# A third tap group on TensorE in a causal convolution, and a bias table written by another queue

## The chip, the cores and the metric

The kernel runs on one core of one Trainium2 chip. The metric is the device time of one execution in microseconds (us); the runs of a kernel are compared by their median. The core has five engines with a queue of instructions each: PE (TensorE, matrix products), DVE (VectorE), ACT (ScalarE), POOL (GpSimd) and SP (which here issues transfers). Each takes its instructions strictly in the order of its queue, and waits on semaphores for what other engines and transfers have to deliver.

## What is computed

Two layers over 256 positions and 2048 channels: a convolution mixer, a feed-forward block with a short causal convolution (FFN), an attention mixer with a relative position bias, and a second FFN. What the change touches is the first mixer and the bias of the attention:

```python
def _conformer_conv(h, w_in, b_in, dw_w, dw_b, ln_g, ln_b, w_out, b_out):
    u = h @ w_in + b_in
    a, gate = jnp.split(u, 2, axis=-1)
    u = a * jax.nn.sigmoid(gate)
    u = _causal_dwconv(u, dw_w, dw_b)            # 31 taps, one filter per channel
    u = jax.nn.silu(_layernorm(u, ln_g, ln_b))
    return u @ w_out + b_out

# in _diff_attention
bucket = _t5_bucket(k_pos[None, :] - q_pos[:, None])
bias = bias_table[:, bucket]
allowed = k_chunk[None, :] <= (q_pos // CHUNK)[:, None]
s = jnp.where(allowed, s + bias[None, :, None], -jnp.inf)
```

All arithmetic is float32. The kernel multiplies by splitting a float32 number into a rounded part (hi) and a rest (lo), and adds three products.

## The kernel before

**Weights.** Every weight matrix is cut into loads of 512 KB. SP's queue brings a load into one of 5 buffers `raw` (L140). ACT writes the rounded copy `hi` (L150), and DVE or POOL the rest `lo` (L152), each with 6 buffers. The splits run four loads ahead of PE. One load feeds one *step* of PE, and a list of steps is the order of the program; `self.at(n, fn)` puts a piece of work n steps later, at the end of that step. Within that, a scheduler that simulates the engines writes the instructions of each queue in order, so the order of the listings below is what runs.

**First mixer** (`conv_module`). 16 tiles of 128 channels; four loads, so four steps, make one tile: 96 matmuls (L217) into a PSUM buffer `pp` (2 of them). When a tile is done, `post` takes it on: DVE multiplies it by the row norm `rstd` into a tile `E` (L436), ACT takes the sigmoid of the gate (L438), DVE multiplies both into the padded tile `cpad` (L440). The 31 taps of the convolution are then shared out. Some go to PE, in groups of four taps: for that the tile must lie in SBUF four times, shifted by one position each. So ACT's queue writes `cpad` to DRAM (`ud`, L452) and reads it back four times (`R`, L456). POOL builds the small diagonal matrices `dg` (L458). `taps` (L475) multiplies them with `R`: 4 matmuls with 32 output rows for each group, side by side in the array, into a PSUM tile `acc` (named s or t). `G` lists how many groups each tile gives to PE: 2 for tiles 0 to 10, then 3, 3, 5, 6; tile 15 goes another way. The taps that are left are steps on DVE (L513), one multiply-add per tap into `acc`, at most six per step of the program and alternating between two tiles where two are open. `dev` (L544) subtracts a mean and keeps the tile for the layernorm, which waits for all 16.

The work on PE of tile i's `taps` is put 4 steps after the tile's end, which is the end of the next tile.

**First FFN, and the set-up of the attention** (`attn_setup`, run at the first step of the FFN). One small matmul makes the bias of all relative positions for 16 heads; DVE copies it to SBUF (L730), and ACT's queue writes it to DRAM 128 times over, 3 MB, as 2048 rows of 384 numbers (`d1`, L732). Each head later reads a skewed window of it (`bm`, L809), from ACT's queue, and POOL sets the masked corner (L810). There are 2 buffers `bm`. In ACT's queue, the reads of the first two heads stand soon after the table's write. In the same stretch the row norm of the FFN is made: POOL takes the power (`rc`, L286), PE turns it into rows (L280), ACT copies them (`rstd`, L348). Each FFN tile is summed up by a copy on ACT (L254) and an addition on DVE (L256), which frees its `pp`.

Of the kernel before, what the change touches and what calls it, by code (L numbers as in the profile page):

```python
# [8 lines left out]
F32 = mybir.dt.float32  # L9
F32R = mybir.dt.float32r  # L10
AF = mybir.ActivationFunctionType
ALU = mybir.AluOpType
AX = mybir.AxisListType
ET = mybir.EngineType
P = 128
S = 256
# [5 lines left out]
MASK = -1.0e30  # L22
# [3 lines left out]
class Cfg:  # L26


    def __init__(self, d, f, kc=4):
        self.D, self.F = d, f  # L30
        self.KT = d // P
        self.FT = f // P
        self.H = d // (2 * HD)
        self.KC = kc
        self.NW = kc * 256
        self.kcs = [(i, kc) for i in range(0, self.KT, kc)]
        full = self.KT // 2
        first = self.FT % full or full
        self.chunks = [(0, first)] + [(i, full) for i in range(first, self.FT, full)]
        self.VK = kc // 2  # L40
        self.NA, self.NB = self.KT + self.KT // 2 + 1, 8

        self.G = [2] * (self.KT - 5) + [3, 3, 5, 6, 0]

        self.ND = 18

# [15 lines left out]
class Builder:  # L62
# [363 lines left out]
    def conv_module(self, nin, nout):  # L426
        c, a = self.c, self.a
# [4 lines left out]

        def post(i, ps):
            with self.tc.high_priority():
                t = self.b2("E")
                nc.vector.tensor_tensor(t, ps[:, :, 0:S], nin["rstd"].unsqueeze(1).to_broadcast([P, 2, S]), ALU.mult)  # L436
                sg = self.b1("G")
                nc.scalar.activation(sg, t[:, 1, :], AF.Sigmoid, bias=self.col("bin", KT + i))  # L438
                u = self.cpad[i % 3]
                nc.vector.scalar_tensor_tensor(u[:, CK - 1:CK - 1 + S], t[:, 0, :], self.col("bin", i), sg, ALU.add,  # L440
                                               ALU.mult)
                if i == KT - 1:
                    nc.scalar.activation(self.c2(), sg[:, 0:2], AF.Silu)
# [11 lines left out]
            for s in range(4):  # L455
# [1 line left out]
            dg = self.ph1.tile([P, 4 * gm, 32], F32, tag="dg", name=self.nm("dg"))[:, :4 * g, :]  # L457
            nc.gpsimd.tensor_tensor(dg, self.cmask.unsqueeze(1).to_broadcast([P, 4 * g, 32]),  # L458
                                    self.col("wq", 4 * sum(c.G[:i]), 4 * g).unsqueeze(2).to_broadcast([P, 4 * g, 32]), ALU.mult)
            self.at(4, lambda: taps(i, u, R, dg))  # L460
            if i == 0:

                for j in range(0, c.ND, 4):
# [255 lines left out]
    def attn_setup(self):  # L719
# [1 line left out]
        nc, c, a = self.nc, self.c, self.a  # L721
        H = c.H
        rb = self.ph2.tile([NB, H], F32, name="rb")
        nc.scalar.dma_start(rb, a["relb"])
        oh = self.b2("Z").rearrange("p a s -> p (a s)")[:NB, :384]
        nc.scalar.dma_start(oh, a["oneh"])
        ps = self.psx("o", [P, 384])
        nc.tensor.matmul(ps[:H, :], rb, oh, start=True, stop=True)
        tb = self.b2("Z").rearrange("p a s -> p (a s)")[:H, :384]
        nc.vector.tensor_copy(tb, ps[:H, :])  # L730
        d1 = self.dr.tile([H, P, 384], F32, name="d1")
        nc.scalar.dma_start(d1, tb.unsqueeze(1).to_broadcast([H, P, 384]))  # L732
        self.bflat = d1.rearrange("h p d -> (h p d)")
        lm = self.c2()
        nc.vector.tensor_tensor(lm[:HD], self.col("lam", 0, 2)[:HD], self.col("lam", 2, 2)[:HD], ALU.mult)
        ps = self.psx("o", [P, 2])
# [12 lines left out]
    def attention(self, nin, nout):  # L749
        c, a = self.c, self.a  # L750
        nc = self.nc
        H, KT = c.H, c.KT
        V, U, O = {}, {}, {}

        def v_group(g, off):
            box = {}
# [47 lines left out]
            self.at(2, lambda: scores(h, q, k, qk))  # L804

        def bias(h):
            bm = self.ph2.tile([P, S], F32, tag="bm", name=self.nm("bm"), bufs=2)
            o = h * P * 384 + P - 1
            nc.scalar.dma_start(bm, self.bflat[o:o + P * 383].rearrange("(p d) -> p d", d=383)[:, :S])  # L809
            nc.gpsimd.memset(bm[0:64, S - 64:], MASK)  # L810
            return bm

        def scores(h, q, k, qk):
            bm = bias(h)
            ps = [self.psx("s", [P, 2, S]) for _ in range(2)]

            comp = [slice(cc * HD, (cc + 1) * HD) for cc in range(2)]
# [64 lines left out]
        for h in range(H):  # L882
            if h % 4 == 0:
                voff = v_group(h // 4, voff)
            off = self.pair(a["w_qk"], off, c.kcs, lambda k: nin["xh"][k], lambda ps, h=h: qk_post(h, ps))
        off = 0
        held = []
        for pr in range(KT // 2):
# [146 lines left out]
```

## Time and profile before

| | |
|---|---|
| median of 3 runs | 2296.82 us (2295.39 to 2298.47) |
| the profiled execution | 2303.02 us, of which the span from first to last instruction is 2300.4 us |
| busy share of the span | PE 97%, DVE 73%, ACT 52%, POOL 12% |
| the chain that ended last | PE 88%, DMA 5%, DVE 4%, issue 1% |

The busy share of PE is an upper bound of the work in it, since matmuls are pipelined and overlap. The chain is followed back from the last instruction to what released each step; its DMA share is time in which the end of the program waited for transfers. "PEclk" is the clock granted to PE as a share of 2.4 GHz.

### The profile page before, as it was taken

What the parts mean: (1) busy time and instruction counts of PE and PEld (TensorE: products, weight loads), DVE (VectorE), ACT (ScalarE), POOL (GpSimd) and SP (SyncE); (2) the same over time, 40 slices, a digit from 0 to 9 for tenths busy, and PEclk for the clock granted to TensorE, in tenths of its full rate; (3) what the DMA queues carried; (4) which work ended last, traced back from release to release, by engine and by line L of the source; (5) the groups of instructions that cost most, each with busy time, mean ns of one, the idle gap of its engine ahead of it and who ended that gap; (6) DMA issues with size and microseconds to landing.
All of it is one profiled execution on the core that took longest, in us unless ns stands there. A gap on an engine that the chain in (4) does not pass through costs nothing.

```text
span 2300.4 us, 34637 instructions
## 1 busy us (share of the span) xinstructions
PE 2224.6 (97%) x13294; PEld 1947.9 (85%) x13294; DVE 1670.9 (73%) x2539; ACT 1205.7 (52%) x1788; POOL 281.4 (12%) x189
## 2 busy tenths in 40 slices
PE   6899799799999999999999999999999999999998
PEld 6788688688888888888888888888888888888887
DVE  5788876577777767677766777677777777676774
ACT  5333265455555555455655555555555555554554
POOL 5678510000000000000111011010000000000002
PEclk9999899899999999999999999999999999999999
DMA  6766356766666666666655555466666666666663
GB/s 230 195 193 190 111 159 179 191 198 187 190 188 188 187 188 190 188 190 188 188 179 159 168 168 166 140 200 183 189 188 190 186 190 185 191 187 190 189 187 100
DMA packets 126885, 417.15 MB, mean 181 GB/s; under 512 B 14176, under 2 KB 28288, under 8 KB 126720
## 3 DMA queue, kind: packets, MB, share of 16 engines
q1 hardware_dynamic: 110736, 398.30, 56.8%
q10 hardware_dynamic: 15984, 16.65, 3.5%
q8 instruction: 104, 1.70, 0.3%
q14 instruction: 61, 0.50, 0.1%
HBM read 407.44 MB, written 7.45 MB: 180 GB/s over the span
## 4 chain that ended last, share of the span: by engine, by line
PE 88%; DMA 5%; DVE 4%; issue 1%; ACTq 0%; ACT 0%; POOL 0%; POOLq 0%; SPq 0%; DVEq 0%
PE pp L226 47%; PE pp L227 24%; PE pp L224 4%; PE pp L217 3%; PE pp L223 2%; DMA R<-ud 2%; DMA ud<-cpad 2%; DMA d<-Z 2%; PE pp L774 1%; PE pp L775 1%; PE pp L776 1%; DVE s L513 1%; DVE cpad L440 1%; PE s L475 0%; ACTq L456 0%
## 5 line engine op out<-in xcount | busy, mean ns | idle before, releaser
L226 PE MATMUL pp<-act,hi 128*128 128x512 f32 x3902 | 1382.9, 396 | 21.1 <-DVE E L256 13.0
L227 PE MATMUL pp<-act,lo 128*128 128x256 f32 x3902 | 1096.5, 281 | 0.0
L150 ACT CAST hi<-raw 128x1024 fp32r<-128x1024 f32 x752 | 787.6, 1049 | 536.0 <-PE pp L226 179.3
L152 DVE TENSOR_TENSOR lo<-raw,hi 128x1024 fp32r<-128x1024 f32 x686 | 844.3, 1231 | 283.0 <-ACT hi L150 281.2
L226 PEld LDWEIGHTS pp<-act,hi 128*128 128x128 f32 x3902 | 733.3, 188 | 182.9 <-DVE E L256 13.3
L227 PEld LDWEIGHTS pp<-act,lo 128*128 128x128 f32 x3902 | 739.1, 189 | 10.4
L226 PE MATMUL pp<-actb,hi 128*128 128x512 f32 x856 | 306.7, 396 | 0.0
L227 PE MATMUL pp<-actb,lo 128*128 128x256 f32 x856 | 240.4, 281 | 0.0
L321 POOL TENSOR_TENSOR ssq<-ssq,Z 128x512 f32<-128x512 f32 x24 | 35.6, 1481 | 1532.1 <-ACT Z L317 1532.0
L217 PE MATMUL pp<-act,hi 128*128 128x256 f32 x1088 | 209.3, 294 | 11.4 <-ACT act L267 6.0
L217 PEld LDWEIGHTS pp<-act,hi 128*128 128x128 f32 x1088 | 178.0, 200 | 19.3 <-DVE act L268 6.6
L226 PEld LDWEIGHTS pp<-actb,hi 128*128 128x128 f32 x856 | 160.6, 188 | 38.3 <-issue 0.6
L152 POOL TENSOR_TENSOR lo<-raw,hi 128x1024 fp32r<-128x1024 f32 x66 | 159.4, 2434 | 56.0 <-ACT hi L150 52.4
L256 DVE TENSOR_TENSOR E<-pp,E 128x512 f32<-128x512 f32 x104 | 71.8, 690 | 128.2 <-ACT E L254 127.9
L227 PEld LDWEIGHTS pp<-actb,lo 128*128 128x128 f32 x856 | 161.5, 189 | 0.2
L217 PE MATMUL pp<-act,lo 128*128 128x256 f32 x544 | 158.4, 291 | 2.8 <-DVE lo L152 2.8
L254 ACT COPY E<-pp 128x512 f32<-128x512 f32 x104 | 60.8, 585 | 186.9 <-PE pp L224 161.6
L370 ACT COPY E<-pp 128x512 f32<-128x512 f32 x109 | 63.9, 586 | 169.5 <-PE pp L224 161.8
L677 DVE SCALAR_TENSOR_TENSOR Y<-fpad,prm,Y 128x256 f32<-128x256 f32 x352 | 146.7, 477 | 0.0
L372 DVE TENSOR_TENSOR x<-pp,x 128x512 f32<-128x512 f32 x101 | 69.7, 690 | 89.4 <-ACT E L370 89.0
L674 ACT ACTIVATE Y<-fpad,prm 128x256 f32<-128x256 f32 x176 | 96.3, 596 | 48.2 <-DVE fpad L670 48.2
L513 DVE SCALAR_TENSOR_TENSOR s<-cpad,cprm,s 128x256 f32<-128x256 f32 x214 | 97.5, 482 | 24.8 <-PE s L475 22.6
(218 smaller groups left out, 1890.8 us busy)
## 6 DMA issues: line engine op xcount, KB each, us to landing
raw<-in_w_up_dram SPq DMA_DIRECT2D x352, 512.0 KB, 4.0
raw<-in_w_down_dram SPq DMA_DIRECT2D x176, 512.0 KB, 4.0
raw<-in_w_in_dram SPq DMA_DIRECT2D x64, 512.0 KB, 4.5
raw<-in_w_qk_dram SPq DMA_DIRECT2D x64, 512.0 KB, 3.6
raw<-in_w_out_dram SPq DMA_DIRECT2D x32, 512.0 KB, 4.1
raw<-in_w_v_dram SPq DMA_DIRECT2D x32, 512.0 KB, 3.7
raw<-in_w_o_dram SPq DMA_DIRECT2D x32, 512.0 KB, 3.7
R<-ud ACTq DMA_DIRECT2D x44, 130.0 KB, 5.1
```

The source lines that it names most:

```text
L150: nc.scalar.copy(hi[:, :n], raw[:, :n])
L152: eng.tensor_tensor(lo[:, :n], raw[:, :n], hi[:, :n].bitcast(F32), ALU.subtract)
L217: nc.tensor.matmul(ps[:, 0:S], w[:, kk, cs], xt[:, x, :], start=(k == first and n == 0), stop=(k == last and n == 2))
L224: nc.tensor.matmul(*main, start=False, stop=True)
L226: nc.tensor.matmul(*main, start=(k == first), stop=False)
L227: nc.tensor.matmul(*corr, start=False, stop=False)
L256: nc.vector.tensor_tensor(t, ps[:, :, 0:S], cs, ALU.add)
L370: nc.scalar.copy(cs, ps[:, :, S:])
L372: nc.vector.tensor_tensor(x, ps[:, :, 0:S], x, ALU.add)
L513: nc.vector.scalar_tensor_tensor(acc, u[:, j:j + S], self.col("cw", i * CK + j), acc, ALU.mult, ALU.add)
L674: nc.scalar.activation(y[:, j, :], u[:, j, FK - 1:], AF.Identity, scale=self.col("fw", ch * FK + FK - 1), bias=self.col("fb", ch))
L677: nc.vector.scalar_tensor_tensor(y[:, j, :], u[:, j, q:q + S], self.col("fw", ch * FK + q), y[:, j, :], ALU.mult, ALU.add)
```

## The change

- `G` becomes 3 for tiles 0 to 12, then 5, 6 (before 2 for tiles 0 to 10): eleven tiles give a third group, four taps, to PE.
- `post` writes the normed projection back into its PSUM tile instead of into `E`; sigmoid and product read it there.
- `taps` of tiles 0 to 13 stand 5 steps after the tile's end, not 4.
- The three transfers of the bias set-up go from ACT's queue to POOL's. The masked corners are written into the table in DRAM, by 16 small transfers of POOL's queue that wait for the table; the 16 memsets of POOL fall away.
- Each head's window `bm` is read by SP's queue, at the first step of the head's own projection, so about one projection before the scores that use it.

```diff
-        self.G = [2] * (self.KT - 5) + [3, 3, 5, 6, 0]
+        self.G = [3] * (self.KT - 3) + [5, 6, 0]
...
         def post(i, ps):
             with self.tc.high_priority():
-                t = self.b2("E")
-                nc.vector.tensor_tensor(t, ps[:, :, 0:S], nin["rstd"].unsqueeze(1).to_broadcast([P, 2, S]), ALU.mult)
+
+                t = ps[:, :, 0:S]
+                nc.vector.tensor_tensor(t, t, nin["rstd"].unsqueeze(1).to_broadcast([P, 2, S]), ALU.mult)
...
-            self.at(4, lambda: taps(i, u, R, dg))
+            self.at(5 if i < KT - 2 else 4, lambda: taps(i, u, R, dg))
...
         rb = self.ph2.tile([NB, H], F32, name="rb")
-        nc.scalar.dma_start(rb, a["relb"])
+        nc.gpsimd.dma_start(rb, a["relb"])
         oh = self.b2("Z").rearrange("p a s -> p (a s)")[:NB, :384]
-        nc.scalar.dma_start(oh, a["oneh"])
+        nc.gpsimd.dma_start(oh, a["oneh"])
...
-        nc.scalar.dma_start(d1, tb.unsqueeze(1).to_broadcast([H, P, 384]))
+        nc.gpsimd.dma_start(d1, tb.unsqueeze(1).to_broadcast([H, P, 384]))
         self.bflat = d1.rearrange("h p d -> (h p d)")
+
+        mk = self.ph2.tile([64, 64], F32, name="mk")
+        nc.gpsimd.memset(mk, MASK)
+        for h in range(H):
+            o = h * P * 384 + P - 1
+            nc.gpsimd.dma_start(self.bflat[o:o + 64 * 383].rearrange("(p d) -> p d", d=383)[:, S - 64:S], mk)
...
         def bias(h):
-            bm = self.ph2.tile([P, S], F32, tag="bm", name=self.nm("bm"), bufs=2)
+            BM[h] = self.ph2.tile([P, S], F32, tag="bm", name=self.nm("bm"), bufs=2)
             o = h * P * 384 + P - 1
-            nc.scalar.dma_start(bm, self.bflat[o:o + P * 383].rearrange("(p d) -> p d", d=383)[:, :S])
-            nc.gpsimd.memset(bm[0:64, S - 64:], MASK)
-            return bm
+            d = nc.sync.dma_start(BM[h], self.bflat[o:o + P * 383].rearrange("(p d) -> p d", d=383)[:, :S])
+            self.tc.keep_in_program_order(d)
 
         def scores(h, q, k, qk):
-            bm = bias(h)
+            bm = BM.pop(h)
...
-            off = self.pair(a["w_qk"], off, c.kcs, lambda k: nin["xh"][k], lambda ps, h=h: qk_post(h, ps))
+            off = self.pair(a["w_qk"], off, c.kcs, lambda k: nin["xh"][k], lambda ps, h=h: qk_post(h, ps),
+                            pre=lambda h=h: bias(h))
```

PE's queue in the middle of the first mixer, before: the last matmuls of one tile (`pp_1581`), the taps of the tile before it, the first matmuls of the next (`pp_1750`).

```order
L217 MATMUL pp_1581<-act_206,hi_1513 128x256 x2
L217 MATMUL pp_1581<-act_206,lo_1514 128x256
L475 MATMUL s_1713<-R_1568,dg_1573 32x256 x8
L217 MATMUL pp_1750<-act_129,hi_1577 128x256 x2
L217 MATMUL pp_1750<-act_129,lo_1578 128x256
```

The same tile's taps (L476 by the new numbering) in the change; `pp_1724` is the tile that before was `pp_1750`, and between its first matmul (`act_129`) and the taps stand 16 rows, which are 24 matmuls.

```order
L217 MATMUL pp_1724<-act_140,lo_1550 128x256
L217 MATMUL pp_1724<-act_140,hi_1549 128x256 x2
L217 MATMUL pp_1724<-act_140,lo_1550 128x256
L476 MATMUL s_1749<-R_1540,dg_1545 32x256 x12
L217 MATMUL pp_1724<-act_150,hi_1604 128x256 x2
```

The taps moved one step of 24 matmuls later, and are 12 matmuls instead of 8. For tile 0 alone they moved by three rows only, since before they already stood in the third tile.

DVE's queue around the end of a tile, before: the normed projection (L436), the product (L440), and tap steps (L513) that alternate between two accumulators.

```order
L513 SCALAR_TENSOR_TENSOR s_1541<-cpad_232,cprm,s_1541 128x256 x7
L436 TENSOR_TENSOR E_1730<-pp_1581,rstd_226 128x512
L513 SCALAR_TENSOR_TENSOR s_1541<-cpad_232,cprm,s_1541 128x256
L513 SCALAR_TENSOR_TENSOR s_1713<-cpad_235,cprm,s_1713 128x256
L513 SCALAR_TENSOR_TENSOR s_1541<-cpad_232,cprm,s_1541 128x256
L440 SCALAR_TENSOR_TENSOR cpad_238<-E_1730,prm,G_1732 128x256
L513 SCALAR_TENSOR_TENSOR s_1713<-cpad_235,cprm,s_1713 128x256
L513 SCALAR_TENSOR_TENSOR s_1541<-cpad_232,cprm,s_1541 128x256
```

The same place in the change (L514 are the tap steps, L437 and L441 the norm and the product).

```order
L514 SCALAR_TENSOR_TENSOR s_1578<-cpad_232,cprm,s_1578 128x256 x15
L437 TENSOR_TENSOR pp_1553<-pp_1553,rstd_226 128x2x256
L514 SCALAR_TENSOR_TENSOR s_1578<-cpad_232,cprm,s_1578 128x256 x2
L441 SCALAR_TENSOR_TENSOR cpad_238<-pp_1553,prm,G_1706 128x256
L514 SCALAR_TENSOR_TENSOR s_1578<-cpad_232,cprm,s_1578 128x256 x2
L545 SCALAR_TENSOR_TENSOR act_1762<-s_1578,prm,mp 128x256
L514 SCALAR_TENSOR_TENSOR s_1749<-cpad_235,cprm,s_1749 128x256 x15
```

A tile's 19 steps now run in one accumulator, 15 before the next tile's end and 4 around it; before, 23 steps ran partly in turn with the next tile's.

ACT's queue at the start of the first FFN, before: the table's write (L732), some splits, the first two window reads (L809), then the copies that free the FFN's `pp` tiles.

```order
L732 DMA d_3950<-Z_3948 2048x1x384
L254 COPY E_4072<-pp_3973 128x512
L150 CAST hi_4116<-raw_4001 128x1024
L150 CAST hi_4138<-raw_4028 128x1024
L739 ACT_TABLE_LOAD
L739 ACTIVATE c_3956<-o_3954 128x2
L150 CAST hi_4160<-raw_4050 128x1024
L150 CAST hi_4201<-raw_4091 128x1024
L809 DMA bm_11322<-d_3950 128x256
L809 DMA bm_11468<-d_3950 128x256
L254 COPY E_4180<-pp_4097 128x512
```

POOL's queue at that place in the change (L733 is the table's write, L286 the row norm's power, L740 the masked corners).

```order
L321 TENSOR_TENSOR ssq_3197<-ssq_3197,Z_3821 128x512
L727 DMA Z_3928<-in_oneh_dram 32x384
L733 DMA d_3934<-Z_3932 2048x1x384
L286 TENSOR_TENSOR rc_3999<-c_4000,mhalf 128x2
L740 DMA d_3934<-mk 64x64 x16
L321 TENSOR_TENSOR ssq_10576<-ssq_10576,Z_10633 128x512
```

The write and everything that waits for it left ACT's queue; in POOL's, the power of the row norm stands right behind the write and ahead of the 16 corners.

## Rows read from the trace of the kernel before

**Rows 1.** The page, the chain that ended last: shares of the span by engine.

```profile
PE 88%; DMA 5%; DVE 4%; issue 1%; ACTq 0%; ACT 0%; POOL 0%; POOLq 0%; SPq 0%; DVEq 0%
```

**Rows 2.** Windows: stretch, length, busy us of PE, PEld, DVE, ACT, POOL, PEclk, DMA, GB/s.

```profile
180.00:240.00 60.00, 54.52 (x487) 51.18 (x485) 50.29 (x104) 21.08 (x24) 51.38 (x27) 1.00 0.68 192
480.00:540.00 60.00, 60.00 (x346) 52.58 (x345) 45.96 (x68) 34.71 (x51) 0.00 (x0) 1.00 0.62 187
1200.00:1300.00 100.00, 100.00 (x573) 83.56 (x572) 74.21 (x158) 56.59 (x122) 9.87 (x15) 1.00 0.56 166
```

**Rows 3.** Waits of PE from 45 to 262 us: total us, times, longest.

```profile
PE s L475 <- DMA R<-ud: 14.0, 7, 4.9
PE t L475 <- DMA R<-ud: 6.0, 3, 2.6
PE s L475 <- issue: 3.2, 1, 3.2
```

**Rows 4.** Windows, tile by tile, where PE's clock was below full.

```profile
58.00:66.00 8.00, 7.24 (x49) 6.05 (x50) 3.43 (x7) 1.04 (x1) 3.93 (x3) 0.63 0.78 248
...
111.00:126.00 15.00, 14.62 (x120) 13.40 (x124) 10.65 (x26) 4.02 (x5) 9.65 (x6) 0.89 0.64 184
...
168.00:182.00 14.00, 13.58 (x108) 13.07 (x109) 10.66 (x24) 3.68 (x4) 9.02 (x6) 0.88 0.65 195
```

**Rows 5.** The chain that ended last, one tile: start us, us, what.

```profile
226.05 0.69 DVE E L436
...
227.57 2.46 DVE cpad L440
230.06 5.11 DMA ud<-cpad
...
236.50 5.34 DMA R<-ud
241.98 3.77 PE s L475 x40
```

**Rows 6.** PE's timeline and chain: taps of two and three groups, cadence, last projection matmul.

```profile
182.62 1.07 PE L475 MATMUL s<-R,dg 128*32 128x256 f32 x16
225.94 1.50 PE L475 MATMUL s<-R,dg 128*32 128x256 f32 x24
257.13 0.28 PE L217 MATMUL pp<-act,lo 128*128 128x256 f32 x1
1129.77 5.74 PE pp L217 x48
```

**Rows 7.** DVE: line L440 (ns min/median/max), and runs of tap steps in its timeline.

```profile
L440 DVE SCALAR_TENSOR_TENSOR cpad<-E,prm,G x16: 478/1362/2453, 44.8 to 263.3; 128x256 f32<-128x256 f32 x16
69.91 10.01 DVE L513 SCALAR_TENSOR_TENSOR s<-cpad,cprm,s 128x256 f32<-128x256 f32 x25
232.30 7.30 DVE L513 SCALAR_TENSOR_TENSOR s<-cpad,cprm,s 128x256 f32<-128x256 f32 x14
```

**Rows 8.** POOL in the first mixer: a wait, and groups of 60 to 240 us by form.

```profile
POOL c L593 <- DVE c L592: 15.0, 1, 15.0
L152 POOL TENSOR_TENSOR lo<-raw,hi 128x1024 fp32r<-128x1024 f32 x48 | 114.9, 2409 | 39.5 <-ACT hi L150 35.9 <-DMA raw<-in_w_in_dram 3.6
```

**Rows 9.** Timelines of ACT, DVE, POOL and PE around the table's write.

```profile
391.33 0.67 ACTq L732 DMA_DIRECT2D d<-Z  x1
427.82 0.59 ACT L254 COPY E<-pp 128x512 f32<-128x512 f32 x1 [25.08 <-DMA d<-Z]
390.76 0.54 DVE L730 COPY Z<-o 16x384 f32<-16x384 f32 x1
400.90 0.70 POOL L286 TENSOR_TENSOR rc<-c,mhalf 128x2 f32<-128x2 f32 x1 [25.41 <-DVE c L285]
404.97 0.61 PE L280 MATMUL o<-ident,rc 128*128 128x128 f32 x4
415.79 0.39 PE L224 MATMUL pp<-actb,hi 128*128 128x512 f32 x1
429.19 0.80 PE L226 MATMUL pp<-act,hi 128*128 128x512 f32 x1 [13.01 <-DVE E L256]
```

**Rows 10.** DMA from 385 to 430 us (write), 397 to 399 and 398.5 to 401.

```profile
d<-Z ACTq DMA_DIRECT2D x1, 3072.0 KB, 35.6
q10 hardware_dynamic: 127, 0.20, 92.8%
raw<-in_w_up_dram SPq DMA_DIRECT2D x2, 512.0 KB, 18.6
```

More of the change, by code (lines that the diff above doesn't have):

```diff
@@ L752, in attention @@
         H, KT = c.H, c.KT
-        V, U, O = {}, {}, {}
+        V, U, O, BM = {}, {}, {}, {}
         def v_group(g, off):
```

## The prediction

> **What bounds the kernel now.** I read the chain that ended last first: 88% of it is PE, so time is won only where PE waits, runs at a lower clock or does more than it must [rows 1]. The windows by stage say where that is. In the FFN and the attention PE is busy in 60.00 of 60 us and 100.00 of 100, at clock 1.00; nothing done to other engines there can help [rows 2]. In the first mixer it is busy in 54.52 of 60 us, while DVE and POOL, at 50.29 and 51.38, are not full either [rows 2]: three engines wait for each other in turn. The waits of PE name the place. From 45 to 262 us it stood idle for 14.0 + 6.0 + 3.2 = 23.2 us, and every one of these eleven waits is ahead of a tile's taps, for the shifted copies R [rows 3]. Its clock adds to that: 0.63, 0.89 and 0.88 of full in three tiles in which PE had just stood still [rows 4], which is 8 x 0.37 + 15 x 0.11 + 14 x 0.12 = 6.3 us of work at full clock that was not done. Together 29.5 us. The second place is the start of the first FFN: after 415.79 + 0.39 us PE is idle for 13.01 us [rows 9].
>
> **The first mixer.** Why R is late can be read along the chain for one tile: norm at 226.05, product until 230.03, ud written by 235.17, four R copies issued and landed by 241.84, taps at 241.98 [rows 5]. That is 15.9 us from the tile's end. Until then PE has one tile of matmuls, 96 x 5.74/48 = 11.5 us, and one set of taps of 1.07 to 1.50 us [rows 6]: 13.0 us at most. It must wait some 2.9 us.
>
> *Later taps.* 24 matmuls more stand ahead of the taps, 24 x 0.12 = 2.9 us, and the set of taps between is 1.50 us: PE gets there 11.5 + 1.5 + 2.9 = 15.9 us after the tile's end. This alone just meets the 15.9 us.
>
> *Norm in PSUM.* The product (L440) reads two tiles in SBUF and takes 478 ns at best, 2453 at worst, 2.46 us in the tile of the chain [rows 5, 7]. A tap step, which also takes one operand from SBUF and one from PSUM, runs in 0.52 us behind its forerunner at the worst [rows 7]. With the projection in PSUM the product is such an instruction; I take 0.48 us, so R comes 2.0 us sooner in such a tile, 13.9 us after its end. The bounds are 0 and 2.0 us. That `pp` is held about 2 us longer costs nothing: the next tile uses the other buffer for 11.5 us.
>
> *What is left of the waits.* 2.0 us of slack stand against more traffic: 192 GB/s with PE busy 54.52 of 60 us becomes about 192 x 60/54.52 = 211 when it is not held [rows 2], and if the 5.11 + 5.34 us of transfers [rows 5] grow in that ratio, 1.0 us of the slack is gone. I leave 0.3 us of wait to each of 11 tiles, 3.3 us. Tile 0 is another matter: its taps moved by three rows, 0.4 us, so of the longest wait, 4.9 us [rows 3], 4.5 us remain, and with them the slow clock behind it, 3.0 us [rows 4]. Gain: 29.5 - 3.3 - 7.5 = 18.7 us. Bounds: 22.0 us without a new wait, and 6.6 if each of 11 tiles waits 1.4 us.
>
> *The third group* costs PE 1.50 - 1.07 = 0.43 us a tile [rows 6], 11 x 0.43 = 4.7 us, all on the path. It takes four tap steps from DVE, but saves DVE little: the 19 that are left all depend on one accumulator, 7.30/14 = 0.52 us each, where alternating ones took 10.01/25 = 0.40 [rows 7]; 19 x 0.52 = 9.9 us. With norm, product and `dev` DVE needs about 11.5 us a tile, and PE 13.0. That is the cover, 1.5 us; were it gone, norms would start late and the taps with them. POOL's larger `dg` (128 numbers more; a split of 1024 takes 2.41 us, so an estimated 0.3 us) hides in the 39.5 us that it was idle ahead of its splits [rows 8]. What follows the last projection matmul (257.13, [rows 6]) moves forward as it is. Sum for the mixer: 18.7 - 4.7 = **14.0 us**, from 2 to 17.
>
> **The start of the FFN.** ACT issues the table's write at 391.33, in 0.67 us. Then its queue comes to the reads of that table, and the copy behind them (L254) starts 25.08 us later than it could, released by the write [rows 9], which takes 35.6 us to land [rows 10]. That copy frees a `pp`, DVE's addition follows, and PE is held 13.01 us; it then restarts with a matmul of 0.80 us against 0.39 [rows 9], and I put 1.5 us of slow clock behind the wait. In the change nothing on ACT waits for the table; PE's next cause of standing still must be looked for. Gain if there is none: **14.5 us**.
>
> What is late next could be POOL. The write now stands in its queue ahead of `rc`, which PE needs for the rows of the norm. Before, POOL took `rc` at 400.90, and PE came to the rows at 404.97 [rows 9]. The table is ready at 391.3, so POOL may spend about 404.97 - 391.3 - 0.8 = 12.8 us on writing out the transfer before PE stands; every us above is lost. No row of before has a transfer issued by POOL. Bounds: 0.67 us, as for ACT [rows 9], and 35.6 us if it were held until all has landed [rows 10]. Nearest is POOL's own pace, 2.41 us for 1024 numbers per partition [rows 8], 2.4 ns each: an estimate of 5 us for 2048 rows at one such unit a row, 19 at four. I take a value under 12.8, cost 0. The Trainium skill speaks against the move: its page "DMA: Bandwidth & Descriptors", section "SWDGE vs HWDGE vs iDMA", says that for transfers issued from GpSimd a program on its cores computes the descriptors, while hardware does it for SP and ACT. The same page of the Trainium skill, section "Anatomy of one DMA", finds that many descriptors come out before their number is felt, by which the cost would be 0; no run here shows either.
>
> The corners come behind `rc`, and POOL has no work from 480 to 540 us [rows 2]. The load of `rb`, new in POOL's queue ahead of the layernorm's power, falls in a wait of 15.0 us [rows 8]. The window reads on SP stand among weight loads and wait for the scores two heads back; weights are split four loads ahead, and PE is never idle there (100.00 of 100, [rows 2]), so 0, and no gain either for ACT and POOL, which are relieved.
>
> **Sum.** 14.0 + 14.5 = 28.5 us. The profiled execution took 2303.0 us, 6.2 above the median of 2296.8; 2303.0 - 28.5 = 2274.5, and on the scale of the median **2268 us**, 1.2% less.
>
> **Rivals.**
>
> *POOL is held by the table's write* for G us, more than 12.8. The time is 2268 + 1.5 + (G - 12.8): 2277 at 20 us, 2292 at 35.6. From 45 us on (22 ns a row) the kernel is slower than before by over 0.2%, which is 4.6 us and about what a measurement can tell; at 60 us it takes 2317. For it: 2048 rows at an unknown price, right ahead of `rc`. Against it: 45 us is longer than the whole transfer now takes, and over nine times POOL's pace per number. 0.12 for 12.8 to 45 us (a third of it within 0.2%), 0.06 for more.
>
> *The wait changes its name.* While the table was written, its queue took 92.8% of the DMA engines, and weight loads landed after 18.6 us [rows 10]. PE did not feel it, since loads already split lasted until it stopped for another reason. If POOL's transfer shuts the loads out for all 35.6 us, the load issued at about 395 lands near 427, its split is ready at 430 and PE, which needs it at about 420, waits 10 us and restarts slowly: some 12 to 13 us of the 14.5 are gone, 2281. Against it: before, the loads came through after 18.6 us. The same page of the Trainium skill has a rule for it, "Issuing engines are not separate DMA queues": moving a transfer to another engine saves only the time of issuing it. By that the FFN gains 0.67 us and the time is 2282; the 25.08 us of ACT were a wait in its queue, not issue, and I hold the rule not to reach it. 0.08.
>
> *The copies stay late.* If ud and R take 3 us longer under the denser traffic, each of 13 tiles waits 1 us more than the slack covers: 13 us, 2281. For it: the DMA engines already show 0.68 of their time busy at 192 GB/s [rows 2]. Against it: the FFN is served at 187 GB/s without a wait of PE. 0.14.
>
> **The numbers.** My forecast has 0.60, with a range of its own of 2260 to 2276. With the rivals: faster by over 0.2% 0.60 + 0.08 + 0.14 + 0.08 = 0.90; within 0.2% 0.04; slower 0.06. The range is 2259 (mixer 17, FFN 14.5, and 6 of the 7.5 us kept for tile 0 gone too) to 2284 (either gain lost nearly whole, or POOL held up to 27 us); above it about 0.1 is left out, below it less.
>
> **What will show it.** Waits of PE ahead of the taps: about 8 us in all instead of 23.2, over half of it in tile 0. The product near 0.48 us. Taps x24 of 1.50 us in nearly every tile, the last projection matmul near 243 us instead of 257. At the FFN no idle PE of 13 us, `rc` at most 4 us later than DVE's input for it, and a POOL row for the write that tells G. Wrong would be: PE idle ahead of the norm's rows (first rival), ahead of a first matmul with a fresh load (second), or still ahead of the taps (third).

## The result, and the profile after

The change takes **2269.08 us** in the median of four runs, the kernel before 2297.64 beside it. Three of the four lie between 2264.77 and 2269.90, with a median of 2268.26; the fourth took 3646.37 at a granted clock of 0.556 and is left out of the ratio, which is 0.987, interval 0.9851 to 0.989. On a second chip it is 0.9866, 0.9847 to 0.9885. It is faster by 1.3%, as forecast in size and sign. But the terms of the sum are not as forecast, and it is worth seeing why two errors gave a right total.

The page of the change, the chain that ended last, shares by engine, where [rows 1] had 88% PE and 5% DMA:

```profile
PE 93%; DVE 2%; DMA 2%; ACT 1%; issue 1%; POOL 0%; SPq 0%; ACTq 0%; POOLq 0%; DVEq 0%
```

Windows of the change, columns as in [rows 2]. The mixer's PE is full now up to the last tiles, and the mixer carries 212 and 213 GB/s, where [rows 2] had 192.

```profile
60.00:120.00 60.00, 59.80 (x551) 55.38 (x550) 50.92 (x107) 22.56 (x27) 50.00 (x27) 1.00 0.73 212
...
180.00:240.00 60.00, 58.25 (x555) 52.94 (x554) 49.49 (x96) 22.67 (x27) 51.16 (x25) 1.00 0.75 213
```

PE's waits ahead of the taps, which in [rows 3] were eleven of 23.2 us, are two of 3.4:

```profile
PE s L476 <- DMA R<-ud: 3.2, 1, 3.2
...
PE s L476 <- issue: 0.2, 1, 0.2
```

PE's longest wait from 45 to 262 us is none of these: 7.35 us ahead of w_out's first matmul, for the end of the layernorm on DVE. It was 7.75 before, so the change leaves it as it was.

PE's timeline of the change. Start, us, what; in brackets idle time ahead and what ended it. Tile 0's taps wait; from the third tile on they come round every 13.14 us, without a wait. The last taps (x48) start at 233.73, right behind the last matmul of the projection, which in [rows 6] stood at 257.13.

```profile
43.09 0.51 PE L217 MATMUL pp<-act,hi 128*128 128x256 f32 x2 [0.78 <-DVE cpad L441]
54.58 1.70 PE L476 MATMUL s<-R,dg 128*32 128x256 f32 x24 [3.19 <-DMA R<-ud]
...
130.44 1.50 PE L476 MATMUL s<-R,dg 128*32 128x256 f32 x24
143.58 1.50 PE L476 MATMUL s<-R,dg 128*32 128x256 f32 x24
...
233.73 2.80 PE L476 MATMUL t<-R,dg 128*32 128x256 f32 x48
```

The product of the change by its line (ns min/median/max), which [rows 7] had at 478/1362/2453:

```profile
L441 DVE SCALAR_TENSOR_TENSOR cpad<-pp,prm,G x16: 472/479/485, 42.6 to 237.5; 128x256 f32<-128x256 f32 x16
```

At the FFN, POOL's timeline has the row that the prediction lacked: writing out the table's transfer holds POOL for 1.03 us. `rc` (L286) is taken right after its input. The corners start when the table has landed.

```profile
365.39 1.03 POOL L733 DMA_DIRECT2D d<-Z  x1 [15.28 <-DVE Z L731]
374.66 0.71 POOL L286 TENSOR_TENSOR rc<-c,mhalf 128x2 f32<-128x2 f32 x1 [8.23 <-DVE c L285]
402.51 4.24 POOL L740 DMA_DIRECT2D d<-mk  x8 [27.14 <-DMA d<-Z]
```

ACT no longer waits for the write in its queue. It waits for a weight load, 11.10 us, and PE's waits from 340 to 440 us are three of 4.1 us in all, in place of the 13.01 of [rows 9]:

```profile
391.25 1.05 ACT L150 CAST hi<-raw 128x1024 fp32r<-128x1024 f32 x1 [11.10 <-DMA raw<-in_w_up_dram]
```

```profile
PE pp L226 <- DVE E L256: 2.1, 1, 2.1
PE pp L226 <- ACT hi L150: 1.2, 1, 1.2
PE pp L227 <- DVE lo L152: 0.8, 1, 0.8
```

The DMA queues of the change from 368 to 382 us and from 384 to 398 (packets, MB, share of 16 engines). q0 is POOL's transfer, q1 carries the weight loads. In the first stretch q1 does not appear at all, though four loads were issued in it; they landed 26.6 us after issue in the median, against 18.6 in [rows 10].

```profile
q0 software_dynamic: 294, 1.35, 97.4%
...
raw<-in_w_up_dram SPq DMA_DIRECT2D x4, 512.0 KB, 26.6
...
q0 software_dynamic: 284, 1.31, 82.3%
q1 hardware_dynamic: 287, 1.04, 18.3%
```

It was like that before too, at first: of ACT's write (q10) and the loads, only the write shows from 395.5 to 409 us. From 411 to 415 the two stand side by side, and there the loads have half of the engines' time:

```profile
q10 hardware_dynamic: 858, 1.32, 92.1%
```

```profile
q1 hardware_dynamic: 234, 0.84, 51.4%
q10 hardware_dynamic: 233, 0.36, 50.4%
```

### The profile page after: what moved, and what is told of

Read it like the earlier page. It is cut to its first block, busy times and chain, and to the rows that moved or that the text cites. A ratio compares the mean times of both kernels' runs of the same rounds, so it can differ in the third digit from the quotient of the medians.

```text
span 2266.3 us, 34758 instructions
## 1 busy us (share of the span) xinstructions
PE 2223.0 (98%) x13382; PEld 1946.8 (86%) x13382; DVE 1649.9 (73%) x2495; ACT 1205.1 (53%) x1788; POOL 292.2 (13%) x193
## 4 chain that ended last, share of the span: by engine, by line
PE 93%; DVE 2%; DMA 2%; ACT 1%; issue 1%; POOL 0%; SPq 0%; ACTq 0%; POOLq 0%; DVEq 0%
PE pp L226 48%; PE pp L227 24%; PE pp L217 7%; PE pp L224 4%; PE pp L223 2%; PE pp L781 1%; PE pp L783 1%; PE pp L782 1%; DMA raw<-in_w_up_dram 1%; PE s L476 1%; PE s L828 0%; PE o L280 0%; PE o L274 0%; PE s L226 0%; PE s L825 0%
## 5 line engine op out<-in xcount | busy, mean ns | idle before, releaser
L227 PEld LDWEIGHTS pp<-act,lo 128*128 128x128 f32 x3902 | 740.5, 190 | 10.1
L217 PE MATMUL pp<-act,hi 128*128 128x256 f32 x1088 | 206.5, 292 | 10.2 <-ACT act L267 6.0
L217 PEld LDWEIGHTS pp<-act,hi 128*128 128x128 f32 x1088 | 175.7, 198 | 17.7 <-ACT act L267 6.0
L217 PE MATMUL pp<-act,lo 128*128 128x256 f32 x544 | 157.4, 289 | 1.0 <-DVE lo L152 1.0
L217 PEld LDWEIGHTS pp<-act,lo 128*128 128x128 f32 x544 | 107.8, 198 | 1.3 <-DVE lo L152 1.3
```

What stands on the lines that cost most here:

```text
L217: nc.tensor.matmul(ps[:, 0:S], w[:, kk, cs], xt[:, x, :], start=(k == first and n == 0), stop=(k == last and n == 2))
L227: nc.tensor.matmul(*corr, start=False, stop=False)
```

## Where the time went, by stretch

Four marks cut a trace into stretches that the parts of the change touch one by one: PE's first norm rows (L280), w_out's first matmul, DVE's copy of the bias table (L730, L731), and the last group of 48 matmuls (L217) of the first FFN on the chain. Differences of their starts, in us:

| kernel | first norm rows at | rows to w_out | w_out to table copy | copy to end of FFN |
|---|---|---|---|---|
| before | 41.71 | 244.8 | 104.2 | 739.0 |
| the change | 38.11 | 222.4 | 104.1 | 732.0 |

So the mixer gave 244.8 - 222.4 = **22.4 us**, the FFN 739.0 - 732.0 = **7.0**. From the end of this FFN to the same group in the second FFN it is 1151.13 before (1129.77 to 2280.90) and 1150.17 after (1096.61 to 2246.78): **1.0 us** from the bias reads. With 0.1 of the third column that is 30.5; the spans differ by 2300.4 - 2266.3 = 34.1. The rest, 3.6 us, is that the first norm rows came at 41.71 in one profile and at 38.11 in the other. Two of the kernels below have the same instructions up to there and show 36.8 and 41.3, so I don't credit it to the change.

## The experiments

All edits are to the change, unless said otherwise. Times are medians; "before" is the kernel before on the same chip.

**The change again.**

> The change, with nothing altered, run again so that the three edits of this call stand beside it on one chip. By both theories its time over that of the kernel before is 0.987 to 0.989, as in its first run (2269.08 over 2297.64); a ratio outside 0.985 to 0.991 would say that a difference of 4 us between edits is within what one chip adds to another.

2267.47 us, before 2298.80, ratio 0.9866. Its stretches are 222.2 and 732.0 us, those of the first profile within 0.2. They can spread more than that: three profiles of one program, below, have 218.5, 220.7 and 220.7 from rows to w_out. A difference of 2 us in that stretch says little by itself.

**Mixer part alone: the bias part undone.**

```diff
...
-        nc.gpsimd.dma_start(d1, tb.unsqueeze(1).to_broadcast([H, P, 384]))
+        nc.scalar.dma_start(d1, tb.unsqueeze(1).to_broadcast([H, P, 384]))
...
-            d = nc.sync.dma_start(BM[h], self.bflat[o:o + P * 383].rearrange("(p d) -> p d", d=383)[:, :S])
+            nc.scalar.dma_start(bm, self.bflat[o:o + P * 383].rearrange("(p d) -> p d", d=383)[:, :S])
+            nc.gpsimd.memset(bm[0:64, S - 64:], MASK)
...
```

> The first mixer's part of the change alone; the bias table is written and read as before. Theory 1 (the mixer gives about 21 us, more than the 14.0 of the prediction, because the waits ahead of the taps vanish but for tile 0's, and the clock with them): 2297.6 - 21 = about 2277 us; waits of PE ahead of the taps about 3.4 us; the 13 us of idle PE at the start of the FFN still there, 25 us on ACT behind the table's write. Rival (the mixer gives the predicted 14.0 and the rest came from the FFN): 2283 us. Rival (the two parts only pay together): above 2290 us.

2277.23 us, before 2301.74, ratio 0.989 [0.9875, 0.9905]. Rows to w_out 223.6, copy to end of FFN 739.7, as before. PE's timeline has the wait of [rows 9] back, to the hundredth:

```profile
403.67 0.80 PE L226 MATMUL pp<-act,hi 128*128 128x512 f32 x1 [13.01 <-DVE E L256]
```

The mixer alone is worth 24.5 us by the medians on that chip and 21.2 by its stretch. My 14.0 was too small.

**Bias part alone: the mixer part undone.**

```diff
-        self.G = [3] * (self.KT - 3) + [5, 6, 0]
+        self.G = [2] * (self.KT - 5) + [3, 3, 5, 6, 0]
...
-                t = ps[:, :, 0:S]
+                t = self.b2("E")
...
-            self.at(5 if i < KT - 2 else 4, lambda: taps(i, u, R, dg))
+            self.at(4, lambda: taps(i, u, R, dg))
```

> The bias part of the change alone; the mixer as before. Theory 1 (the FFN's start gives about 7 us, since PE then waits some 4 us for weight loads held up by the table's write and runs slow after that): 2290 us, PE idle about 4 us there, weight loads landing up to 28 us after issue. Rival (the predicted 14.5 us): 2283 us. Rival (issuing from another queue saves the time of issue alone): 2297 us.

2289.43 us, before 2301.74, ratio 0.9951 [0.9939, 0.9964]. Rows to w_out 247.0, copy to end of FFN 728.9. The three waits of PE at the FFN are there without the mixer part, for the same three instructions, 1.6, 1.4 and 0.8 us. PE's clock stays full here, and the stretch gains 739.0 - 728.9 = 10.1 us. In the change slow clock follows the waits. Windows of the change (length, PE busy, PEclk, DMA share, GB/s):

```profile
397.00:401.00 4.00, 2.06 (x10) 0.94 0.97 188
401.00:405.00 4.00, 4.00 (x15) 0.64 1.03 412
405.00:409.00 4.00, 1.94 (x7) 0.79 0.89 308
409.00:413.00 4.00, 4.00 (x20) 0.78 0.62 173
```

Busy time by what is missing of the clock, that is 0.12 + 1.44 + 0.41 + 0.88 = 2.9 us, and the stretch gains 7.0.

By the medians the two parts are worth 24.5 and 12.3 us, 36.8 together, where both in one give 28.6 to 31.3. Some 3 us of that is the FFN, 10.1 against 7.0. The rest is not settled: the kernel before has 2301.74 on this chip, 2297.64 and 2298.80 beside the change.

**Two groups again, later taps and norm in PSUM kept.**

```diff
-        self.G = [3] * (self.KT - 3) + [5, 6, 0]
+        self.G = [2] * (self.KT - 5) + [3, 3, 5, 6, 0]
```

> The changed kernel with two tap groups for tiles 0 to 10 again (three for tiles 11 and 12), later taps and norm in PSUM kept. Theory (a third group is work of PE on the path, 0.43 us a tile, and DVE's 23 steps still fit in a tile because two accumulators alternate at 0.40 us): 11 x 0.43 = 4.7 us faster than the change, 2264 us; tile to tile about 12.7 us on PE instead of 13.14; no more waits ahead of the taps. Rival (the third group relieves DVE, whose chain of tap steps would otherwise hold the norm: 23 x 0.52 + 1.7 = 13.7 us a tile): 13 tiles x 0.5 us, 2275 us, with DVE busy to the end of each tile and PE waiting ahead of the taps again.

2263.80 us, before 2301.74, ratio 0.9831 [0.9818, 0.9845]. Rows to w_out 219.7, where the change has 222.4: the third group costs time, and without it the tiles between the first and the last still come round without a wait. PE's timeline shows its price by the tile, 12.70 us from taps to taps against 13.14:

```profile
117.93 1.07 PE L476 MATMUL t<-R,dg 128*32 128x256 f32 x16
130.63 1.07 PE L476 MATMUL s<-R,dg 128*32 128x256 f32 x16
```

11 x 0.44 = 4.8 us; some of it comes back as a longer wait ahead of tile 0's taps (3.9 us) and of the last ones (1.4). The FFN, 729.3 here, added 2.7 us more, in a stretch that the edit does not touch.

**The table written in pieces.**

```diff
-        nc.gpsimd.dma_start(d1, tb.unsqueeze(1).to_broadcast([H, P, 384]))
+        def piece(x):
+            self.tc.keep_in_program_order(nc.sync.dma_start(d1[:, 8 * x:8 * x + 8, :],
+                                                            tb.unsqueeze(1).to_broadcast([H, 8, 384])))
+        for x in range(16):
+            self.at(4 * x + 4, lambda x=x: piece(x))
...
-        for h in range(H):
+        def corner(h):
...
+        for h in range(H):
+            self.at(70 + h, lambda h=h: corner(h))
```

> The changed kernel with the table's write cut into 16 pieces of 192 KB, issued on SP's queue among the weight loads, one piece after each four loads; the corners are set when all pieces are in. Theory (the 4.1 us of idle PE and the slow clock at the start of the FFN come from weight loads that land late while the table's write has the DMA engines): no idle PE there, clock 1.00, weight loads landing within about 8 us, 7 us faster than the change: 2262 us. Rival (PE idles there because ACT and DVE come late with the norm's rows and their backlog, whatever the loads do): idle stays near 4 us, 2269 us.

2261.72 us, before 2301.74, ratio 0.9825 [0.9812, 0.9839]. Copy to end of FFN is 724.2 us, 14.8 less than before. PE does not wait; window from 360, loads from 364 to 440 us:

```profile
360.00:440.00 80.00, 80.00 (x459) 69.32 (x458) 58.86 (x87) 46.79 (x66) 0.71 (x1) 1.00 0.64 200
```

```profile
raw<-in_w_up_dram SPq DMA_DIRECT2D x27, 512.0 KB, 4.0
```

The same 3 MB, in pieces between the weight loads, hardly delay a load: 4.0 us to landing in the median, instead of 26.6. That the late loads are what is left of the stall in the change is shown by this run. Which part of the edit does it is not: it cuts the write, and it also takes it from POOL's queue to that of the loads. The write in one piece on SP's queue was not tried.

**Norm into SBUF again, later taps and three groups kept.**

```diff
-                t = ps[:, :, 0:S]
-                nc.vector.tensor_tensor(t, t, nin["rstd"].unsqueeze(1).to_broadcast([P, 2, S]), ALU.mult)
+                t = self.b2("E")
+                nc.vector.tensor_tensor(t, ps[:, :, 0:S], nin["rstd"].unsqueeze(1).to_broadcast([P, 2, S]), ALU.mult)
```

> The change, but with the normed projection in an SBUF tile again; three groups and taps five steps later stay. Theory (both the later place and the quicker product were needed): the product goes back to some 1.4 us in the mean and 2.46 us in bad tiles, R is ready up to 15.9 us after its tile's end, and with three groups PE comes to the taps 13.14 + 2.9 = 16.0 us after it; so half of the tiles wait, 0.3 to 1 us each, some 5 us in all with the slow clock behind them, 2274 on the scale where the change has 2269. Rival (the later place alone was enough): no wait ahead of the taps beyond tile 0's 3 us, and the change's own time within 2 us.

2275.18 us, before 2298.80, ratio 0.9899 [0.988, 0.9917]; the change on that chip 2267.47. Rows to w_out 228.3, 6 us more than the change. The size is as expected, the place is not: most of it is tile 0, and only two more tiles wait. The product by its line, and PE's waits:

```profile
L441 DVE SCALAR_TENSOR_TENSOR cpad<-E,prm,G x16: 473/1862/2733, 41.0 to 242.8; 128x256 f32<-128x256 f32 x16
```

```profile
PE s L476 <- DMA R<-ud: 6.8, 1, 6.8
PE t L476 <- DMA R<-ud: 2.9, 2, 2.0
```

**Taps 4 steps after the tile again, norm in PSUM and three groups kept.**

```diff
-            self.at(5 if i < KT - 2 else 4, lambda: taps(i, u, R, dg))
+            self.at(4, lambda: taps(i, u, R, dg))
```

> The change, but with the taps of every tile 4 steps after its end, as before; norm in PSUM and three groups stay. Theory (both were needed): R is ready about 13.9 us after the tile's end, PE comes there after 11.5 + 1.5 = 13.0 us, so nearly each of 12 tiles waits 0.5 to 1 us and restarts slowly now and then; some 10 us of waits and clock, 2277 on the scale where the change has 2269. Rival one (the quicker product alone was enough): within 2 us of the change. Rival two (the later place alone did it): 20 us of waits as before, 2290 or more.

2279.04 us, before 2298.80, ratio 0.9912 [0.9894, 0.993]. Rows to w_out 231.3, 9 us more than the change (its first norm rows were also 3.4 us later). Four waits ahead of the taps, 8.8 us, not a small one in each tile; and the wait ahead of the last tile's product (L485) is 3.9 instead of 1.6:

```profile
PE s L476 <- DMA R<-ud: 7.0, 3, 3.6
PE s L485 <- DVE cpad L441: 3.9, 1, 3.9
PE t L476 <- DMA R<-ud: 1.8, 1, 1.8
```

Together the two runs say: either edit alone, with three groups, leaves 9 to 10 of the 23.2 us of waits, both leave 3.4. They are not a sum. Each moves most tiles over the same edge, and the second only takes the tiles that the first leaves. What the third group alone does to the waits (it brings PE to the taps 0.43 us later) was not tried.

**Two groups and the table in pieces**, the two edits above together.

> The change, but with two groups for tiles 0 to 10 as before, and with the bias table written in 16 pieces of 192 KB by SP's queue, one every four steps, and the masked corners a step apart after it. Theory: the two edits act in different stretches and add, 5 us (two groups) and 7 us (spread write), 2257 on the scale where the change has 2269; no PE wait over 1 us at the start of the first FFN, and taps of 1.07 us. Rival: with two groups the tiles come round 0.4 us sooner and DVE has four tap steps more, so its queue makes the norms late; waits ahead of the taps of 0.3 us or more in each of 11 tiles take the 5 us back, 2262.

2258.74 us, before 2298.80, ratio 0.9825 [0.9806, 0.9844]; 8.7 us under the change on that chip, of the 12 expected. The FFN gives what it should (724.2), rows to w_out is 218.5, 3.7 less. By the medians the third group costs less than its 4.8 us on PE, so both were run side by side.

**The table in pieces, with three groups and with two, on one chip.**

> The spread write with three groups, again, so that two groups and the later place of tile 0 stand beside it on one chip. Both theories: 0.981 to 0.984 of the kernel before, 14 to 15 us from the table's copy to the end of the FFN less than before.

> The spread write with two groups, again. Theory (the third group only costs PE, 11 x 0.43 us, of which the trace of the first run shows 3.8 us between the first norm rows and w_out's first matmul): 3 to 5 us under the spread write with three groups. Rival (what two groups save comes back as waits and slow clock): within 2 us of it.

2261.00 us (2260.53 to 2262.44) with three groups, 2259.56 (2255.99 to 2261.85) with two, before 2298.70; ratios 0.9831 and 0.9822. Rows to w_out 224.0 and 220.7. Over all profiles the five kernels with three groups and taps at step 5 that keep the norm in PSUM have 222.2 to 224.0, the four with two groups (that of the next experiment among them) 218.5 to 220.7. The traces say 3 us, this pair of medians 1.4 with ranges that overlap. The next experiment is the same program as that with two groups, on the same chip; the nine runs of both have a median of 2258.34, 2.7 under the three groups. That the third group gains nothing is shown, how much it costs is not settled between 1 and 4 us.

**Tile 0's taps later still**, at 6 steps, on the kernel with two groups and the table in pieces:

```diff
-            self.at(5 if i < KT - 2 else 4, lambda: taps(i, u, R, dg))
+            self.at(6 if i == 0 else 5 if i < KT - 2 else 4, lambda: taps(i, u, R, dg))
```

> The spread write with two groups, and the taps of tile 0 alone 6 steps after its end, not 5. Theory (the wait that is left in the mixer is that of tile 0, 3.9 us for its R copies and 2.5 us of slow clock behind it, and one step more is 24 x 0.12 = 2.9 us): the wait falls to about 1 us, 3 to 5 us are gained, 2254 where the spread write with two groups has 2259. Rival (DVE takes it back): DVE waited 11.8 us for those taps already, ahead of its own tap steps; 2.9 us more make it late with the next norms, PE waits ahead of the next taps instead, and the time is within 1 us of the other, or above.

2258.34 us, before 2298.70, ratio 0.9819 [0.9805, 0.9833]. This run tells nothing of the theory: the scheduler left tile 0's taps at the same place in PE's queue. It is a third run of the same program in all but buffer numbers, and so shows the spread at the start: the first norm rows at 41.27 us, against 36.77 and 37.03, behind the same instructions.

**Tile 0's taps at 8 steps**, which does move them, 33 matmuls later. In this kernel five tap steps of tile 0 read the padded tile after tile 3's product has been written over it; the number and the size of the instructions are the same.

> The spread write with two groups, and the taps of tile 0 put 8 steps after its end, which moves them on PE behind 33 more matmuls, to the end of the third tile; 6 steps had left them where they were. Theory (what is left of waiting in the mixer is tile 0's, 3.9 to 5.4 us ahead of its taps and 2.5 us of slow clock behind): 33 x 0.12 = 3.9 us of work stand ahead now, the wait falls under 1.5 us, and 3 to 5 us are gained: 0.980 to 0.981 of the kernel before, where the spread write with two groups has 0.9822 and 0.9825. Rival (DVE takes it back): its 23 tap steps of tile 0 wait for those taps, so they come 3.9 us later less the wait that is gone, the next norms and taps are late in turn, and PE waits there, 2 us or more in the next two tiles; 0.982 to 0.984.

2258.55 us, before 2302.78, ratio 0.9811 [0.9798, 0.9824]. The interval holds the theory's range and the lowest fifth of the rival's, so the time does not decide, but the trace does. Rows to w_out is 220.1, among the 218.5 to 220.7 of the taps at 5 steps. PE's timeline:

```profile
57.05 1.07 PE L476 MATMUL s<-R,dg 128*32 128x256 f32 x16
66.47 1.93 PE L476 MATMUL s<-R,dg 128*32 128x256 f32 x16 [5.28 <-DMA R<-ud]
```

Tile 0 waits no longer, tile 1 waits 5.3 us for its own copies, where it had not waited with the taps at 5 steps. So the wait is not tile 0's: at the start both tiles' copies are late, and moving tile 0's taps only hands the wait on. My rival named DVE, and that is not what the row shows (DVE holds PE once, later, for 1.7 us ahead of the last taps). The copies land a median of 7.2 us after issue there, against 5.34 in the chain of [rows 5]. A part of it is ACT's queue: tile 1's product ends at 47.44 us, but its write stands behind tile 0's four reads, which wait for tile 0's write until 48.48, and is issued at 50.60. Another order of that queue was not tried, nor whether the loads that fill the buffers ahead make the copies late.

## Why the prediction was right, and where it was not

**The forecast** was 2268, range 2259 to 2284; both medians, 2269.08 and 2267.47, lie within 1.1 us of it. The sum of 28.5 us stands against 28.6 and 31.3 by the medians and 30.4 by the stretches. That it fits is luck: the mixer's term was 8.4 us too small, that of the FFN 7.5 too large, and the two errors have nothing in common. What was right is the mechanism in the mixer, and that the reads of the table held ACT.

**The mixer: 14.0 forecast, 22.4 found, above its upper bound of 17.** From the first norm rows to the last taps it is 257.33 - 41.71 = 215.6 before and 233.73 - 38.11 = 195.6 after, 20.0 us; the other 2.5 come after that. By the steps of the prediction:
- *What is left of the waits.* I left 3.3 us to 11 tiles: they have 0.2. The traffic rose to 212 and 213 GB/s, about as worked out (211), but the slack was enough.
- *Tile 0* was to keep 4.5 us idle and 3.0 of slow clock; it keeps 3.2 and 1.7. This was also the step that set the upper bound too low: I counted those 7.5 us as fixed.
- *The slow clock.* I read three tiles, 6.3 us; there was a fourth, at 242 to 246 us, behind the wait in the chain of [rows 5]. Summed over windows of 2 us, it is 7.2 before and 1.7 after.
- *Norm in PSUM.* The product takes 0.479 us, as taken. "That `pp` is held about 2 us longer costs nothing" holds for all tiles but the first, where PE waits 0.78 us for it (the row at 43.09 above).
- *The third group* costs 0.43 us a tile, as taken. Together: 23.2 - 3.4 - 0.8 idle, 7.2 - 1.7 clock, less 4.7, is 19.8 of the 20.0.
- *"What follows moves forward as it is"* was wrong by 2.5 us. Behind the last taps PE waits for the last tile's product, 3.8 us before and 1.6 after, and DVE reaches that late. PE's waits, then DVE's timelines before and after, tell why:

```profile
PE s L484 <- DVE cpad L440: 3.8, 1, 3.8
```

```profile
PE s L485 <- DVE cpad L441: 1.6, 1, 1.6
```

```profile
252.13 2.19 DVE L559 TENSOR_TENSOR act<-act,act 128x512 f32<-128x512 f32 x1
254.25 2.90 DVE L560 TENSOR_TENSOR lnsq<-lnsq,Z 128x512 f32<-128x512 f32 x1
257.06 2.60 DVE L568 TENSOR_TENSOR M<-act 128x256 f32<-128x256 f32 x1
259.59 2.56 DVE L568 TENSOR_TENSOR M<-lnsq 128x256 f32<-128x256 f32 x1
```

```profile
231.22 0.69 DVE L560 TENSOR_TENSOR act<-act,act 128x512 f32<-128x512 f32 x1
232.38 2.40 DVE L561 TENSOR_TENSOR lnsq<-lnsq,Z 128x512 f32<-128x512 f32 x1 [0.47 <-ACT Z L552]
234.71 0.41 DVE L569 TENSOR_TENSOR M<-act 128x256 f32<-128x256 f32 x1
...
235.64 1.98 DVE L569 TENSOR_TENSOR M<-lnsq 128x256 f32<-128x256 f32 x1
```

These sums read two SBUF tiles. POOL was splitting weights all through the first stretch. In the second it has gaps, from 231.36 to 231.83 and from 234.23 to 234.70:

```profile
251.36 10.50 POOL L152 TENSOR_TENSOR lo<-raw,hi 128x1024 fp32r<-128x1024 f32 x4 [6.01 <-ACT hi L150]
```

```profile
228.95 2.41 POOL L152 TENSOR_TENSOR lo<-raw,hi 128x1024 fp32r<-128x1024 f32 x1 [1.59 <-ACT hi L150]
231.83 2.40 POOL L152 TENSOR_TENSOR lo<-raw,hi 128x1024 fp32r<-128x1024 f32 x1 [0.46 <-ACT hi L150]
234.70 2.63 POOL L152 TENSOR_TENSOR lo<-raw,hi 128x1024 fp32r<-128x1024 f32 x1 [0.47 <-ACT hi L150]
```

The sum at 231.22, of which most falls in a gap, takes 0.69 us, and that at 234.71, which begins within 0.01 us of a split, takes 0.41. The six others take 1.98 to 2.90, and each of them ends shortly after a split of POOL: 0.55 us after it with 512 columns, 0.28 or 0.29 with 256.

The same explains the product: 1862 ns in the median with two SBUF operands, 479 with one. One product before and POOL's split beside it, then the same in the change:

```profile
67.81 2.17 DVE L440 SCALAR_TENSOR_TENSOR cpad<-E,prm,G 128x256 f32<-128x256 f32 x1
```

```profile
67.34 2.36 POOL L152 TENSOR_TENSOR lo<-raw,hi 128x1024 fp32r<-128x1024 f32 x1 [1.03 <-ACT hi L150]
```

```profile
62.80 0.48 DVE L441 SCALAR_TENSOR_TENSOR cpad<-pp,prm,G 128x256 f32<-128x256 f32 x1
```

```profile
62.33 2.39 POOL L152 TENSOR_TENSOR lo<-raw,hi 128x1024 fp32r<-128x1024 f32 x1 [1.31 <-ACT hi L150]
```

Before, the product begins 0.47 us into the split and ends at 69.98, 0.28 after it; in the change it begins as far into one and is done long before its end. That holds for all of them. In the three profiles that read the product from `E` (before, the bias part alone, norm into SBUF again), each of the 40 products of more than 0.5 us ends 0.28 or 0.29 us after an instruction of POOL. In the change 15 of 16 run beside a split of POOL, and none takes more than 0.485. So the price of the second SBUF operand is what is left of POOL's instruction, here up to one split of 2.4 us.

The Trainium skill has it as a rule ("SBUF — State Buffer", section "Who interferes with whom"): a DVE instruction with two SBUF inputs contends with a GpSimd instruction that reads SBUF, one with at most one does not (outside modes of DVE that use two ports). These rows agree, and with it I should have taken the 2.0 us as sure, not as a bound.

**The FFN: 14.5 forecast, 7.0 found.** The 14.5 was rightly sized: before, PE lost 13.0 us of waiting and, summed over windows of 2 us, 1.7 to the clock, and the table in pieces gives 14.8 back. The step that failed is "cost 0" for what is late next. I gave it to POOL, whose time G was the open price. G is 1.03 us, below even the lower estimate of 5, `rc` was on time, and that rival falls. What came was the other rival, in half: the loads land after 26.6 us, not 18.6, PE waits 4.1 us and loses 2.9 to the clock. I had given it 0.08 and priced it at 12 to 13 us; it takes 7.5.

That the write shuts the loads out at first is not new with POOL's queue: ACT's write did so for as long, some 14 us, and PE, which stood still for ACT's copy first, did not feel it. New is what comes after that, where the loads have 18.3% of the engines' time beside POOL's write and had 51.4% beside ACT's. Against this rival I had held that before the loads came through after 18.6 us. That took for granted that a write from another queue leaves the loads the same share.

I had weighed the rule of the Trainium skill by which another issuing engine saves only the time of issuing ("DMA: Bandwidth & Descriptors", section "Issuing engines are not separate DMA queues"); by it the FFN would gain 0.67 us. It gained 7.0, since ACT's 25.08 us were a wait in its queue. The 7.5 that are missing were lost where two queues share the DMA engines, of which the same section speaks.

**The attention** was put at 0 and gives 1.0 us: from the end of the first FFN to that of the second it is 1150.2 with the bias part alone and 1151.2 with the mixer part alone. Which of the relieved queues it is was not tried.

**The start.** The profile of before lay 6.2 us above the median. Some 3.6 of that may be its late first norm rows; when these come in the runs without a profile is not known. The forecast does not hang on it, since the sum was set back to the median.

## What to carry to other kernels

When a transfer is moved off a queue because others wait behind it there, ask next what its bytes do to the loads: cut in pieces and put between the loads on their own queue, the same 3 MB left PE without a wait, where in one piece on POOL's they still cost 7.8 us. When several engines wait in turn, edits that shorten the loop are not added up; work out by tile which of them takes the tile over the edge, and price the clock with the wait. And let an instruction of DVE that others wait for read one operand from PSUM while POOL works: with both in SBUF it ended here only after POOL's instruction.

## What was not expected of the hardware

- One instruction holds POOL for 1.03 us for a transfer of 2048 rows, and eight transfers of 64 rows hold it for 4.2 us.
- A product on DVE with both operands in SBUF ended 0.28 us after POOL's instruction in 40 of 40 cases of more than 0.5 us; with one operand in PSUM none of 16 took more than 0.485.
- While the table's write and the weight loads stood side by side, the loads first got nothing for some 14 us, from either queue. Then write and loads had as many packets each: 284 and 287 with POOL's write, for 82.3% and 18.3% of the engines' time, so that its packets take some 4.5 times as long; 233 and 234 with ACT's, for half of the time each. The Trainium skill ("DMA: Bandwidth & Descriptors", section "Queues, rings and completion order") says that an engine takes the queues in turn by packets; the later stretches agree, the first do not, and no run here shows why.
- The first norm rows come at 36.8 to 38.1 us in nine profiles and at 40.0 to 41.7 in five, and between two programs that differ in buffer numbers alone by 4.5; three programs that were profiled twice had the same value within 0.3. The cause is open.
